# Output projection by seven block products with adding loads, one list schedule behind the attention, and a plain first feed-forward pair

## The chip, the cores and the metric

The kernel runs on one core of a Trainium2 chip. The metric is the device time of one execution in microseconds, as the median of several runs. The engines are TensorE (PE in the profile, with its weight loads as PEld), VectorE (DVE), ScalarE (ACT), GpSimd (POOL) and SyncE (SP), which here only issues transfers.

## The reference

One block of a network with two mixers, a 1024 x 1024 input in float32: an input projection, an mLSTM and a sparse attention side by side, and then what the change touches:

```python
branch = jnp.einsum('btnw,nwd->btnd', ys, w_branch[l])      # 2 branches, 512 -> 1024
gates = jax.nn.sigmoid(merge.reshape(B, T, N_BRANCH, D_MODEL))
mixed = jnp.sum(gates * branch, axis=2)
h = h + mixed @ w_out[l]                                    # 1024 x 1024
f = rms_norm(h, g_norm_ffn[l])
h = h + (jax.nn.silu(f @ w_gate[l]) * (f @ w_up[l])) @ w_down[l]   # 1024 -> 2816 -> 1024
return rms_norm(h, g_final)
```

## The kernel before

Every float32 product is made of three: both operands are split into a rounded part and a rest (hi by a copy on ACT, lo by a subtraction on another engine), and `mm3` (L350 to L353) issues hi x hi, hi x lo and lo x hi into one PSUM tile of 128 x 512. A plain product over 1024 inputs is thus 8 x 3 = 24 matmuls; a block product over 512 inputs is 12.

The attention ends at about 689 us of the trace, in the same way before and after the change. What follows it stood in two parts. The first is written out in order: three last tiles of the merge gates (`merge_tile`, matmuls on tile `d`), loads of the two mixers' results `y` and their splits (`load_y`), and the branch products (tile `br`, eight steps d of two halves and two branches; L1865 multiplies a product with its gate, L1873 adds the two branches, L347 and L348 split the sum into `UTH` and `UTL`, the eight mixed tiles). Their weights come through `Stream` (`ws`), which splits a weight tile on ACT (L331) and DVE or, for the merge gates, GpSimd (L333).

The second part is a list schedule (`Plan`): steps are recorded with the engines that may run them, an estimated cost and the buffers that they read and write. Then a greedy planner takes, again and again, the step that can start first, among the next few steps (`LOOK`) of each engine's list, and issues it. The costs are only the planner's; they set the order in which each engine's instructions stand in the program. Recorded there were: 16 output products `wout` (half of the columns, row block i; 24 matmuls each, and each reads all eight mixed tiles), each followed by the addition of x, a store of h and a square on ACT; `feats`, the normalisation of a row block (`rstd_steps`, small operations of one column, then L2000 with three operands) and its transposes (L2037); `fsplit`, the operands of the feed-forward's block products; `product`, the gate and up products by seven block products for each pair of 128-column tiles (m is a pair of tiles, q = 1, 2, 6, 7, 5, 4, 3 the product), the first pair with its four earliest products in halves of 256 columns; the down projection, by seven block products in two groups, with `combine` adding the products up on DVE or GpSimd; and a final stage (L2334), which does the last tiles of the down projection plainly, adds, normalises and stores. `ew` (L1893) records every element-wise operation, so in the profile all of them have that line, and they are told apart by their tiles; `act` is L1896, `dma` L1903. In the block products of gate and up one operand sum is made by a load that adds to what lies there (`sums`, L2109, issued by GpSimd), 256 KB each.

## Time and profile before

| | us |
|---|---|
| median of 3 runs | 1563.68 (1561.17 to 1564.3) |
| profiled execution | 1560.07 |
| its span in the trace | 1558.3 |
| TensorE busy | 1519.5 (98%), 7714 matmuls |
| DVE busy | 1159.7 (74%) |
| ACT busy | 782.0 (50%) |
| GpSimd busy | 182.2 (12%) |
| TensorE's part of the chain that ended last | 87% |

The part behind the attention is the last 869 us of the span. A stretch is read by comparing the busy time of TensorE with its length; a name such as `PS<-UTH,wh` gives the tile written and the tiles read. In the profile one matmul of 128x512 is shown with 0.39 us, which overlaps its neighbours; what it costs is the distance from one start to the next.

### The profile page before, as it was taken

How to read it: one execution, taken by the hardware profiler on the slowest of the kernel's cores; microseconds unless marked ns; L12 is line 12 of the kernel's file. 1: busy time of each engine (PE TensorE's matmuls, PEld its weight loads, DVE VectorE, ACT ScalarE, POOL GpSimd, SP SyncE). 2: the span in 40 equal slices, each digit the busy share in tenths (PEclk: the TensorE clock that was granted, in tenths of full speed). 3: DMA queues.
4: the chain of work that ended last, by engine and by line, in shares of the span. 5: the costliest groups of instructions: out<-in, count | busy, mean ns of one | idle time of the engine just before them, and what ended most of it. 6: DMA issues, size and time to landing. Idle time of an engine off the chain costs nothing.

```text
span 1558.3 us, 22160 instructions
## 1 busy us (share of the span) xinstructions
PE 1519.5 (98%) x7714; PEld 1283.8 (82%) x7714; DVE 1159.7 (74%) x2444; ACT 782.0 (50%) x1668; POOL 182.2 (12%) x235
## 2 busy tenths in 40 slices
PE   6999999999999999999999999999999999999997
PEld 5877888888989888987878888888888888888876
DVE  6978888875988688856564586666666666978996
ACT  5325665653888688865443353333333333454443
POOL 2000000013121412111000051000000000000120
PEclk9999999999999999999999999999999999999999
DMA  8324655489241925236455244444454443660202
GB/s 275 121 76 127 231 171 169 158 242 258 42 114 41 183 42 116 46 110 218 139 182 203 68 127 117 111 112 110 108 165 117 115 111 122 249 217 1 108 1 108
DMA packets 185496, 207.66 MB, mean 133 GB/s; under 512 B 10584, under 2 KB 145142, under 8 KB 185384
## 3 DMA queue, kind: packets, MB, share of 16 engines
q1 hardware_dynamic: 157272, 184.63, 37.4%
q0 software_dynamic: 27824, 20.96, 9.6%
q8 instruction: 61, 1.00, 0.3%
q10 hardware_dynamic: 288, 0.66, 0.1%
q14 instruction: 51, 0.42, 0.1%
HBM read 155.78 MB, written 58.29 MB: 137 GB/s over the span
## 4 chain that ended last, share of the span: by engine, by line
PE 87%; DVE 7%; DMA 3%; ACT 2%; issue 1%; SPq 0%; POOL 0%; DVEq 0%; ACTq 0%; POOLq 0%
PE PS L352 15%; PE PS L353 15%; PE PS L351 15%; PE bk L351 5%; PE bk L352 5%; PE bk L353 5%; PE T L1524 4%; PE obank L1546 2%; PE obank L1544 2%; PE d L351 2%; PE d L353 2%; PE d L352 2%; PE br L353 2%; PE br L352 2%; PE br L351 1%
## 5 line engine op out<-in xcount | busy, mean ns | idle before, releaser
L1893 DVE TENSOR_TENSOR sl<-PS,sl 128x512 f32<-128x512 f32 x182 | 123.1, 688 | 96.2 <-PE PS L353 93.5
L1533 DVE TENSOR_TENSOR TL<-T,TH 128x512 fp32r<-128x512 f32 (+1 forms) x184 | 103.3, 582 | 28.7 <-ACT TH L1529 27.8
L1529 ACT ACTIVATE TH<-T 128x512 fp32r<-128x512 f32 (+1 forms) x184 | 90.4, 510 | 26.2 <-PE T L1524 23.1
L1893 DVE TENSOR_TENSOR sl<-sl,sl 128x512 f32<-128x512 f32 (+1 forms) x113 | 77.7, 695 | 17.1 <-ACT sl L1896 13.3
L1896 ACT ACTIVATE sl<-sl 128x512 f32<-128x512 f32 (+1 forms) x85 | 53.2, 630 | 72.0 <-PE PS L352 46.8
L1896 ACT ACTIVATE wh<-sl 128x512 fp32r<-128x512 f32 x61 | 38.4, 630 | 80.4 <-PE PS L352 66.0
L351 PE MATMUL bk<-UTH,op 128*128 128x512 f32 x192 | 77.4, 403 | 0.0
L353 PE MATMUL bk<-UTH,op 128*128 128x512 f32 x192 | 75.0, 391 | 0.0
L352 PE MATMUL bk<-UTL,op 128*128 128x512 f32 x192 | 74.9, 390 | 0.0
L351 PE MATMUL d<-UTH,whi 128*128 128x512 f32 x176 | 71.8, 408 | 1.8 <-ACT mg L1396 1.1
L353 PE MATMUL d<-UTH,wlo 128*128 128x512 f32 x176 | 69.2, 393 | 0.8 <-POOL wlo L333 0.8
L352 PE MATMUL d<-UTL,whi 128*128 128x512 f32 x176 | 69.0, 392 | 0.0
L351 PE MATMUL PS<-q 128*128 128x512 f32 x172 | 66.9, 389 | 0.0
L352 PE MATMUL PS<-q 128*128 128x512 f32 x172 | 66.9, 389 | 0.0
L353 PE MATMUL PS<-q 128*128 128x512 f32 x172 | 66.9, 389 | 0.0
L1896 ACT ACTIVATE q<-sl 128x512 fp32r<-128x512 f32 x74 | 43.5, 625 | 45.7 <-PE PS L352 30.0
L351 PE MATMUL bk<-T,op 128*128 128x512 f32 x144 | 58.1, 404 | 0.0
L353 PE MATMUL bk<-T,op 128*128 128x512 f32 x144 | 56.3, 391 | 0.0
L352 PE MATMUL bk<-T,op 128*128 128x512 f32 x144 | 56.2, 390 | 0.0
L1558 POOL DMA_DIRECT2D d_yn<-os x32 | 31.9, 997 | 174.1 <-DMA d_yn<-os 51.1
L1893 DVE TENSOR_TENSOR wh<-sl,wh 128x512 fp32r<-128x512 f32 x59 | 40.4, 684 | 15.3 <-ACT wh L1896 15.3
L353 PE MATMUL br<-YH,wlo 128*128 128x512 f32 x128 | 49.9, 390 | 1.6 <-POOL wlo L333 1.6
(1378 smaller groups left out, 4898.3 us busy)
## 6 DMA issues: line engine op xcount, KB each, us to landing
rp<-in_w_in SPq DMA_DIRECT2D x22, 512.0 KB, 4.7
ra<-in_w_gate SPq DMA_DIRECT2D x22, 512.0 KB, 3.9
d_gu<-sl SPq DMA_DIRECT2D x44, 256.0 KB, 2.1
q<-d_mg SPq DMA_DIRECT2D x32, 256.0 KB, 3.1
d_rep<-d_row SPq DMA_DIRECT2D x8, 960.0 KB, 7.4
sl<-d_gu SPq DMA_DIRECT2D x15, 512.0 KB, 4.1
sl<-in_w_down SPq DMA_DIRECT2D x15, 512.0 KB, 4.7
ra<-in_w_up SPq DMA_DIRECT2D x11, 512.0 KB, 3.6
```

The costliest lines, as they stand in the source:

```text
L351: nc.tensor.matmul(ps, ah, bh, start=first, stop=False)
L352: nc.tensor.matmul(ps, ah, bl, start=False, stop=False)
L353: nc.tensor.matmul(ps, al, bh, start=False, stop=last)
L1524: nc.tensor.transpose(pt[:, z, P * r:P * r + P], e, ident)
L1529: nc.scalar.activation(hl[0][:, 0:m], pt[:, 0:m], AF.Copy)
L1533: nc.vector.tensor_tensor(hl[1][:, 0:m], pt[:, 0:m], cast32(hl[0])[:, 0:m], ALU.subtract)
L1544: nc.tensor.matmul(po, vv, th[:, z, :], start=(st[1] == 0), stop=False)
L1546: nc.tensor.matmul(po, vv, tl[:, z, :], start=False, stop=(st[1] == st[2]))
L1558: low_half.append(lambda: nc.gpsimd.dma_start(dst, half(1), accum_op=ALU.add))
L1893: return pl.step(alts, lambda e: ENG[e].tensor_tensor(out_(), x(), y(), alu), reads, writes, **kw)
L1896: return pl.step((("ACT", cost),), lambda e: nc.scalar.activation(out_(), x(), fn), reads, writes, **kw)
```

## The change

All that follows the attention is recorded in one `Plan`: merge tiles, loads of y, branch products, output projection, feed-forward. The planner looks further ahead (60 steps on PE in place of 10, 140 on DVE in place of 60), a step on PE is planned 1 us later than its operands, and element-wise steps go to DVE alone, apart from `combine` and the multiplies named below. The weights of merge and branches have their lo part made on DVE. The mixed rows stay whole (float32) in `UTH`.

The output projection is made by seven block products (`wprod(q, j)`, q = 1, 2, 6, 5, 3 and then 7 and 4 by turns, j the pair of row blocks; 28 steps of 12 matmuls). Its weight sums are made in memory order by loads: four plain ones (`wo_load`) and five adding ones on GpSimd (`wo_add`), 1 MB each, in three tiles (`quad_0` to `quad_2` in the order below); the sums of the mixed rows (`s1` to `s4`) are made on DVE; x comes by 16 adding loads of 256 KB on GpSimd (`xadd`), where it was loaded and added on DVE. The rows are normalised in pairs, and for 12 of the 16 tiles the multiplication with the gain is split: a scaled copy on ACT and a multiply on GpSimd. The first gate/up pair is made by eight plain products (`plain`), even rows first; the sums for the odd rows' block products follow (`row1_rest`).

```diff
-    pl = Plan([PS[:, n, :] for n in range(8)])
-    ENG = {"DVE": nc.vector, "Pool": nc.gpsimd}
-    ANY = (("DVE", 600.0), ("Pool", 1230.0))
-    V, SUM = (("DVE", 600.0),), (("DVE", 600.0),)
...
+    pl = Plan([PS[:, n, :] for n in range(8)], {"PE": 60, "SP": 60, "ACT": 100, "DVE": 140, "Pool": 60}, 1000.0)
+    ENG = {"DVE": nc.vector, "Pool": nc.gpsimd}
+    V = SUM = ANY = (("DVE", 670.0),)
+    V2 = (("DVE", 1140.0),)
+    BOTH = (("DVE", 670.0), ("Pool", 1230.0))
...
+    def dma(dst, src, reads=(), writes=(), kb=256.0, **kw):
+        pl.step((("SP", 400.0),), lambda e: nc.sync.dma_start(dst(), src()), reads, writes, kb=kb, nd=1, **kw)
+
+    def dma_add(dst, src, writes, lat):
+        pl.step((("Pool", 1000.0),), lambda e: nc.gpsimd.dma_start(dst(), src(), accum_op=ALU.add), (), writes, lat=lat)
...
+        if t:
+            rb = pl.buf(keys_of(raw), True)
+            if t > 1:
+                dma(lambda: v8(f32(raw)), lambda: src, (), [rb], kb=512.0)
+        hb, lb = pl.buf(keys_of(hi), True), pl.buf(keys_of(lo), True)
+        if t:
+            act(1000.0, lambda: slot_ap(hi, F32R), lambda: f32(raw), AF.Copy, [rb], [hb])
+            ew(V2, lambda: slot_ap(lo, F32R), lambda: f32(raw), lambda: cast32(slot_ap(hi, F32R)), ALU.subtract, [rb, hb], [lb])
+        wb[t] = [hb, lb]
...
+            m = [mxb.setdefault((d, r, h), pl.buf(ukeys("H", [d], [r], [2 * h, 2 * h + 1]), True)) if b == 0 else mxb[d, r, h] for r in range(2)]
+            if b == 0:
+                ew(V, lambda h=h: mixed(d, h), lambda ps=ps: ps.ap, lambda g=g: g.ap, ALU.mult, [ps, g], m)
+            else:
+                ew(V, lambda g=g: g.ap, lambda ps=ps: ps.ap, lambda g=g: g.ap, ALU.mult, [ps], [g])
+                ew(V, lambda h=h: mixed(d, h), lambda h=h: mixed(d, h), lambda g=g: g.ap, ALU.add, [g], m)
...
+    def wo_add(n, kh, ch):
+        b = WT[n]
+        dma_add(lambda: b.ap, lambda: wo_blk(kh, ch), [b], 12000.0)
...
+    HOME = {1: "L", 2: 0, 6: 8, 5: 0, 3: 8, 7: 20, 4: 0}
...
+    def prep_b(q, n):
+        t = WT[n]
+        for kk in range(4):
+            prepare(q, "B", kk, lambda kk=kk: t.ap[:, kk, :], [t])
...
+    def s3(kk):
+        ew(V, lambda: mx(kk, 1), lambda: mx(kk, 0), lambda: mx(kk, 1), ALU.subtract, mxs(kk, 0), mxs(kk, 1))
+
+    def s2(kk):
+        b = s2b[kk] = fpiece(28 + kk // 2, kk % 2)
+        stt_neg(lambda: four(b.ap), lambda: mx(kk, 1), lambda: mx(4 + kk, 1), mxs(kk, 1) + mxs(4 + kk, 1), [b])
+
+    def s1(kk):
+        b = s2b[kk]
+        stt_neg(lambda: mx(kk, 0), lambda: four(b.ap), lambda: mx(kk, 0), [b], mxs(kk, 0))
+
+    def s4(kk):
+        b = s2b[kk]
+        stt_neg(lambda: mx(4 + kk, 0), lambda: four(b.ap), lambda: mx(4 + kk, 0), [b], mxs(4 + kk, 0))
...
+    def wprod(q, j, ps, first=True, last=True):
+        def go(e):
+            for kk in range(4):
+                aa, bb = opb[q, "A", kk][2], opb[q, "B", kk][2]
+                js = slice(P * j, P * j + P)
+                mm3(ps.ap, aa(0)[:, js], aa(1)[:, js], bb(0), bb(1), first and kk == 0, last and kk == 3)
+        pl.step((("PE", 12 * 226.7),), go, [x for w in "AB" for kk in range(4) for x in opb[q, w, kk][:2]], [ps])
...
-    def wout(hf, i):
-        ps = pl.buf()
-        cs = slice(P * i, P * i + P)
-
-        def go(e):
-            for k in range(KT):
-                wh, wl = wod[k - k % 2] if hf == 0 else (b.ap for b in wo1[k - k % 2:k - k % 2 + 2])
-                mm3(ps.ap, UTH[:, k, cs], UTL[:, k, cs], wh[:, k % 2, :], wl[:, k % 2, :], k == 0, k == KT - 1)
-        pl.step((("PE", 5184.0),), go, [mixb[i]] + ([wo0], wo1)[hf], [ps])
-        return ps
...
+    def xadd(r, c, j):
+        b = xp[r, c, j]
+        i = 2 * j + r
+        src = a["x"][P * i:P * i + P, 512 * c:512 * c + 512]
+        dma_add(lambda: b.ap, lambda: src, [b], 6000.0)
...
+            stt(lambda b=b: b.ap, lambda b=b: b.ap, i, lambda c=c: gFb.ap[:, c, :], [gFb], [b], r == 0 or j < 2)
...
+    def row0(j):
+        for c, pt in enumerate(rows_f(0, j)):
+            b = xp[0, c, j]
+            fsplit(1 + c, j, lambda pt=pt: four(pt.ap), [pt])
+            act(587.0, lambda b=b: b.ap, lambda pt=pt: pt.ap, AF.Copy, [pt], [b])
...
+    def plain(m, r, c):
+
+        ps = pl.buf()
+        fq = ((1, 2), (8, 3))[r]
+
+        for kh in range(2):
+            def go(e, kh=kh):
+                o, (fh_, fl_) = OB[m, kh, c], blk(fq[kh])
+                for k in range(4):
+                    mm3(ps.ap, o.ap[:, 0, P * k:P * k + P], o.ap[:, 1, P * k:P * k + P], fh_[:, k], fl_[:, k], kh + k == 0, kh * k == 3)
+            pl.step((("PE", 12 * 226.7),), go, [OB[m, kh, c]] + [fsb[fq[kh], j] for j in range(4)], [ps])
...
-    seq = [(0, 1), (0, 2), (1, 1), (1, 2)]
-    seq += [(m, q) for q in (6, 7, 5, 4, 3) for m in (0, 1)]
-    seq += [(m, q) for m in range(2, NM) for q in (1, 2, 6, 7, 5, 4, 3)]
+    seq = [(m, q) for m in range(2, NM) for q in (1, 2, 6, 7, 5, 4, 3)]
...
+        if d == 0:
+            wo_load(0, 0, 0)
+            wo_load(1, 1, 1)
+            wo_load(2, 1, 0)
+        if d == 2:
+            for kk in range(4):
+                prep_a(1, kk)
+            prep_b(1, 0)
+            wo_add(0, 0, 1)
+            wo_add(0, 1, 1)
+            for kk in range(4):
+                s3(kk)
...
+    p1b += [x for w in "AB" for kk in range(4) for x in opb[1, w, kk][:2]]
+    b1 = bank()
+    for j in range(4):
+        wprod(1, j, b1[j])
+    for j in range(4):
+        out_piece(1, 0, j)
+        act(587.0, lambda d=xp[1, 0, j]: d.ap, lambda s=b1[j]: s.ap, AF.Copy, [b1[j]], [xp[1, 0, j]])
+    for kk in range(4):
+        s2(kk)
+        s1(kk)
+    prep_ab(2, 2)
+    wo_load(2, 0, 0)
+    wo_add(2, 0, 1)
+    b2 = bank()
+    for j in range(4):
+        wprod(2, j, b2[j])
+        out_piece(0, 0, j)
+        post(0, 0, j, b2[j], (1, 0))
+        xadd(0, 0, j)
...
+    prep_ab(6, 0)
+    wo_add(0, 1, 0)
+    plain_ops(0)
...
+    b6 = bank()
+    for j in range(4):
+        wprod(6, j, b6[j])
+        post(1, 0, j, b6[j])
+        stored(0, 0, j)
+    prep_ab(5, 2)
+    b5 = bank()
+    for j in range(4):
+        wprod(5, j, b5[j])
+        out_piece(1, 1, j)
+        post(1, 1, j, b5[j], (1, 0), 3)
+        xadd(1, 0, j)
+    prep_ab(3, 1)
+    wo_add(1, 0, 1)
+    b3 = bank()
+    for j in range(4):
+        wprod(3, j, b3[j])
+        out_piece(0, 1, j)
+        post(0, 1, j, b3[j], (1, 1), 2)
+        xadd(0, 1, j)
+        xadd(1, 1, j)
...
+    for j in range(4):
+        stored(0, 1, j)
+    for j in range(4):
+        b7 = pl.buf()
+        wprod(7, j, b7)
+        post(1, 1, j, b7, None, 2)
+        post(1, 0, j, b7)
+        stored(1, 1, j)
+        row0(j)
+        b4 = pl.buf()
+        wprod(4, j, b4)
+        post(1, 0, j, b4)
+        stored(1, 0, j)
+    plain_ops(1)
+    for j in range(4):
+        row1(j)
+    pl.boost = 80
+    for m in range(2):
+        for c in range(2):
+            plain(m, 0, c)
+    pl.boost = 0
+    for m in range(2):
+        for c in range(2):
+            plain(m, 1, c)
...
-                into(ANY, g(d), g(d), g(x), ALU.add, [g(x)])
-
+                into(BOTH, g(d), g(d), g(x), ALU.add, [g(x)])
```

GpSimd from the attention's last store on, before: weight splits of the merge tiles (`wlo`) and then element-wise work of the first feed-forward products (`wl`, `wh`).

```order
L1558 DMA d_yn_150<-os_7523 64x2x128
L333 TENSOR_TENSOR wlo_7568<-raw_6897,whi_7567 128x1024
L333 TENSOR_TENSOR wlo_7653<-raw_7548,whi_7652 128x1024
L333 TENSOR_TENSOR wlo_7734<-raw_7631,whi_7733 128x1024
L1893 TENSOR_TENSOR wl_8415<-ra_8411,wl_8415 128x512
L1893 TENSOR_TENSOR wh_8414<-ra_8412,wh_8414 128x512
L1893 TENSOR_TENSOR wh_8413<-ra_8410,wh_8413 128x512
```

After:

```order
L1560 DMA d_yn_150<-os_7523 64x2x128
L1875 DMA quad_0_float_7549<-in_w_out 128x4x512 x3
L1875 DMA quad_2_float_7569<-in_w_out 128x4x512
L1875 DMA UTL_float_8419<-in_x 128x512 x5
L1875 DMA quad_1_float_7564<-in_w_out 128x4x512
L1875 DMA UTL_float_8419<-in_x 128x512 x11
L1862 TENSOR_TENSOR UTL_float_8419<-UTL_float_8419,ra_7545 128x512 x12
```

GpSimd's splits are gone; its queue now holds the adding loads, those of the weights among those of x, and then the 12 multiplies with the gain.

DVE where the branches end and the output projection begins, before: the multiplies of the last mixed tile (`q_5_0`), a split of w_out's weights, the last mixed tile's addition and split, and splits of the other half of w_out.

```order
L1865 TENSOR_TENSOR q_5_0_7535<-br_8364,q_5_0_7535 128x512
L1865 TENSOR_TENSOR q_5_0_7535<-br_8378,q_5_0_7535 128x512
L333 TENSOR_TENSOR q_3_5_8354<-raw_8392,q_1_5_8353 128x1024
L1873 TENSOR_TENSOR q_5_0_7535<-q_5_0_7535 128x512
L348 TENSOR_TENSOR UTL<-q_5_0_7535,UTH 128x512
L1893 TENSOR_TENSOR sl_10_8468<-ra_8410,sl_8_8464 128x1024
```

After (`quad_3` holds gates, `UTH_float` the mixed rows, `ra` an operand sum, `sl_11` and `sl_18` the second product's lo parts):

```order
L1862 TENSOR_TENSOR quad_3_float_7598<-PS,quad_3_float_7598 128x512
L2039 SCALAR_TENSOR_TENSOR UTH_float_7797<-ra_7544,UTH_float_7797 128x4x128
L1862 TENSOR_TENSOR UTH_float_7797<-UTH_float_7797,quad_3_float_7598 128x512
L1862 TENSOR_TENSOR sl_11_float32r<-UTH_float_7797,sl_7_float32r 128x512
L1862 TENSOR_TENSOR quad_3_float_7598<-PS,quad_3_float_7598 128x512
L1862 TENSOR_TENSOR sl_18_float32r<-quad_2_float_7569,sl_14_float32r 128x512
L1862 TENSOR_TENSOR UTH_float_7797<-UTH_float_7797,quad_3_float_7598 128x512
L1862 TENSOR_TENSOR sl_18_float32r<-quad_2_float_7569,sl_14_float32r 128x512
```

The first product's operands stand earlier in the list; between the last mixed tiles' multiplies and additions there are now sums and splits for the second product.

## Rows read from the trace of the kernel before

**Rows 1.** The page: busy time of the engines over the span, TensorE's granted clock in 40 slices (9 is full), and the engines' shares of the chain that ended last.

```profile
PE 1519.5 (98%) x7714; PEld 1283.8 (82%) x7714; DVE 1159.7 (74%) x2444; ACT 782.0 (50%) x1668; POOL 182.2 (12%) x235
...
PEclk9999999999999999999999999999999999999999
...
PE 87%; DVE 7%; DMA 3%; ACT 2%; issue 1%; SPq 0%; POOL 0%; DVEq 0%; ACTq 0%; POOLq 0%
```

**Rows 2.** Busy time by stretch behind the attention: the stretch and its length, then busy us (and instructions) of PE, PEld, DVE, ACT and POOL, the granted clock, DMA share and GB/s.

```profile
688.00:720.00 32.00, 30.69 (x137) 24.96 (x136) 14.39 (x17) 16.58 (x24) 5.76 (x3) 1.00 0.72 245
720.00:740.00 20.00, 18.41 (x82) 14.92 (x81) 11.23 (x14) 9.69 (x16) 2.36 (x1) 1.00 0.71 211
...
810.00:820.00 10.00, 7.83 (x35) 6.18 (x34) 8.18 (x10) 5.34 (x9) 0.00 (x0) 1.00 0.64 205
820.00:902.00 82.00, 82.00 (x384) 68.42 (x383) 42.26 (x90) 26.07 (x59) 5.18 (x4) 1.00 0.38 131
902.00:947.00 45.00, 42.90 (x245) 37.20 (x244) 39.34 (x63) 21.84 (x40) 23.93 (x17) 1.00 0.53 129
947.00:1328.00 381.00, 381.00 (x1683) 315.48 (x1682) 245.14 (x382) 127.07 (x207) 23.10 (x18) 1.00 0.43 118
1328.00:1475.00 147.00, 147.00 (x650) 121.74 (x649) 132.09 (x216) 69.89 (x122) 5.10 (x4) 1.00 0.39 144
1475.00:1512.00 37.00, 35.21 (x155) 28.50 (x153) 37.00 (x51) 14.45 (x26) 14.38 (x10) 1.00 0.07 29
1512.00:1550.30 38.30, 36.83 (x161) 30.15 (x161) 26.20 (x74) 14.83 (x40) 0.56 (x1) 1.00 0.23 83
1550.30:1558.30 8.00, 0.00 (x0) 0.00 (x0) 3.37 (x9) 0.93 (x3) 1.94 (x2) 0.72 0.35 131
```

**Rows 3.** TensorE's waits from 690 us to the end: the waiting matmul's tile and line, what it waited for, us in total, times, and the longest.

```profile
PE PS L351 <- DVE q L1865: 2.2, 1, 2.2
PE PS L352 <- DVE q L1893: 1.9, 1, 1.9
PE br L353 <- POOL wlo L333: 1.6, 1, 1.6
PE PS L352 <- DVE wl L1893: 1.2, 1, 1.2
PE PS L352 <- DVE UTL L1893: 1.2, 2, 1.0
PE PS L2037 <- DVE sl L1893: 0.9, 2, 0.5
PE d L353 <- POOL wlo L333: 0.8, 1, 0.8
```

**Rows 4.** Timeline of TensorE in the first gate/up pair, the products in halves of 256 columns: start, duration, instruction.

```profile
911.02 0.28 PE L353 MATMUL PS<-UTH,wh 128*128 128x256 f32 x1
911.14 0.28 PE L351 MATMUL PS<-UTH,wh 128*128 128x256 f32 x1
```

**Rows 5.** Loads: the group of adding loads on GpSimd (busy, mean ns of one, idle ahead of it), the medians from issue to landing of those and of a plain 512 KB load of w_out (count, KB, us), and two stretches of 1 us in which an adding load lands (columns as in rows 2).

```profile
L2109 POOL DMA_DIRECT2D sl<-in_w_up x11 | 14.6, 1331 | 157.7 <-DMA sl<-in_w_up 157.7
...
sl<-in_w_up POOLq DMA_DIRECT2D x11, 256.0 KB, 5.0
ra<-in_w_out SPq DMA_DIRECT2D x4, 512.0 KB, 4.8
...
1012.00:1013.00 1.00, 1.00 (x6) 0.84 (x5) 0.96 (x2) 0.00 (x0) 0.00 (x0) 1.00 0.93 131
1013.00:1014.00 1.00, 1.00 (x6) 0.84 (x5) 0.85 (x2) 0.63 (x1) 0.00 (x0) 1.00 1.13 141
```

**Rows 6.** Timeline of DVE and GpSimd in the down projection's additions: start, duration of the group, instruction and count; and the group of GpSimd's additions over the whole run (busy, mean ns, idle before).

```profile
1478.16 4.44 DVE L1893 TENSOR_TENSOR acc<-acc 128x512 f32<-128x512 f32 x4
1479.77 1.68 POOL L1893 TENSOR_TENSOR acc<-acc,acc 128x512 f32<-128x512 f32 x1 [0.63 <-DVE acc L1893]
1508.26 2.47 DVE L1893 TENSOR_TENSOR acc<-acc,PS 128x512 f32<-128x512 f32 x4
1509.01 2.55 POOL L1893 TENSOR_TENSOR acc<-acc,acc 128x512 f32<-128x512 f32 x2 [11.46 <-DVE acc L1893]
...
L1893 POOL TENSOR_TENSOR acc<-acc,acc 128x512 f32<-128x512 f32 x10 | 13.6, 1373 | 56.2 <-DVE acc L1893 56.2
```

**Rows 7.** The entry of the output projection: a load of w_out in the chain that ended last, and the split that DVE ran on landing (timeline).

```profile
802.01 6.94 DMA raw<-in_w_out
808.74 2.55 DVE L333 TENSOR_TENSOR q<-raw,q 128x1024 fp32r<-128x1024 f32 x2 [1.01 <-ACT q L331]
```

**Rows 8.** Timeline behind the last matmul: the last addition, its square, the first and the last small operations of the normalisation, and the last multiply.

```profile
1550.23 0.69 DVE L1893 TENSOR_TENSOR acc<-acc,PS 128x512 f32<-128x512 f32 x1 [1.32 <-PE PS L353]
1551.01 0.63 ACT L1979 ACTIVATE sq<-acc 128x512 bf16<-128x512 f32 x1 [0.73 <-DVE acc L1893]
1551.77 0.49 DVE L1987 TENSOR_TENSOR sml<-sml 128x1 f32<-128x1 f32 x1 [0.85 <-ACT sq L1979]
1553.17 0.15 DVE L367 TENSOR_SCALAR sml<-sml 128x1 f32<-128x1 f32 x1
1553.55 1.41 DVE L2000 SCALAR_TENSOR_TENSOR ra<-acc,sml,sl 128x512 f32<-128x512 f32 x2
```

More of the change, by code (lines that the diff above doesn't have):

```diff
@@ new lines, in body, with own, quad, slot_ap @@
+    WHI = [two(whi0), wpl.tile([P, 2, 512], F32R, name="wh1", tag="whi", bufs=2)]
+    WLO = [two(wlo0), wpl.tile([P, 2, 512], F32R, name="wl1", tag="wlo", bufs=2)]
+    def own(key, pool, shape, dt, tag):
+        if key not in held or held[key].dtype != dt:
+            held[key] = pool.tile([P, *shape], dt, name=f"{tag}_{len(held)}_{dt.name}", tag=tag, bufs=1)
+        return held[key]
+    def quad(n, dt):
+        return own(("q", n), q2p if n < 4 else q1p, (4, 512), dt, f"quad{n}")
+    def slot_ap(n, dt):
+        if n < 8:
+            return own(n, q2p, (2, 512), dt, f"sl{n}")
+        if n < 28:
+            q = quad(n // 2 - 4, dt)
+            return q[:, 2 * (n % 2):2 * (n % 2) + 2, :]
+        if n < 31:
+            return RAW[n - 28]
+        return (WHI, WLO)[(n - 31) // 2][(n - 31) % 2]
@@ new lines, in big, with f32, keys_of, half_keys @@
+    def big(n, dt):
+        return own(("u", n), utp, (16, 512), dt, ("UTH", "UTL")[n])
+    def f32(n):
+        return slot_ap(n, F32)
+    def keys_of(n):
+        if 8 <= n < 28:
+            return [("Q", 2 * n - 16 + z, j) for z in range(2) for j in range(4)]
+        return [(n, z) for z in range(2)]
+    def half_keys(n, z):
+        k = keys_of(n)
+        h = len(k) // 2
+        return k[h * z:h * z + h]
+    def slot_buf(n, dt=F32):
+        return pl.buf(keys_of(n), make=lambda: slot_ap(n, dt))
@@ new lines, in piece, with pieces, fpiece, ukeys @@
+    def piece(c):
+        n, z = divmod(c, 2)
+        return pl.buf(half_keys(n, z), make=lambda: slot_ap(n, F32)[:, z, :])
+    def pieces(n):
+        return [piece(2 * n + z) for z in range(2)]
+    def fpiece(n, z):
+        return pl.buf(half_keys(n, z), make=lambda: f32(n)[:, z, :])
+    def ukeys(e, ks, rs, js):
+        return [("U", e, k, r, j) for k in ks for r in rs for j in js]
+    pl = Plan([PS[:, n, :] for n in range(8)], {"PE": 60, "SP": 60, "ACT": 100, "DVE": 140, "Pool": 60}, 1000.0)
@@ new lines, in body @@
+    for t in range(2):
+        weights(t, w_src(t))
+    for k in range(2):
+        yload(k)
+    merge(MG1)
+    weights(2, w_src(2))
+    yload(2)
+    merge(MG1 + 1)
+    weights(3, w_src(3))
+    yload(3)
+    merge(MG1 + 2)
+    weights(4, w_src(4))
+    for k in range(4, 8):
+        yload(k)
+    for d in range(0, 8, 2):
+        for z in range(2):
+            branch(d + z, 0)
+        for z in range(2):
+            branch(d + z, 1)
+            if d + z < 6:
+                weights(5 + d + z, w_src(5 + d + z))
+        if d == 0:
[10 more added lines that the diff above has]
+                s3(kk)
```

516 lines of the change are left out of this document (272 added, 244 removed).

## The prediction

> **What bounds the kernel now.** I read the page's first lines, then busy time by stretch of the part that the change rewrites, then TensorE's waits in it, and last the timeline at three places. TensorE bounds: it is busy 1519.5 of 1558.3 us at a granted clock of full speed in every slice, and 87% of the chain that ended last lies on it [rows 1]. DVE has 74%. So only two things can move the end: how many matmuls TensorE has to do, and how long it stands idle between the attention's last matmul (about 689.4) and the last matmul of all (1550.2). The stretches [rows 2] show that most of that part is full: 82.00 of 82, 381.00 of 381 and 147.00 of 147 us. Idle lies at six places: 1.31 us at 688 to 720 (0.47 of it the end of the attention, which stays), 1.59 at 720 to 740, 2.17 at 810 to 820, 2.10 at 902 to 947, 1.79 at 1475 to 1512 and 1.47 at 1512 to 1550. That is 10.4 in all, 9.9 without the attention's end, and the list of waits names 9.8 of it [rows 3]: the largest is the first output product waiting for a split of the weights or of the mixed rows (2.2), then an operand sum late in the down projection (1.9), then two waits on GpSimd's weight split (1.6 and 0.8). A last 8 us lie behind the last matmul.
>
> **TensorE's own work.** 1683 matmuls of 128x512 fill 381.00 us [rows 2], so one takes 0.2264 to 0.2267 us; a 256-wide one follows the next at 0.12 [rows 4]. The output projection goes from 16 products of 24 matmuls to 28 steps of 12: 384 to 336, -48 x 0.2267 = -10.9 us. The first gate/up pair goes the other way: before 14 block products, four of them in two 256-wide halves (96 x 0.12 = 11.5 us) and ten whole (120 x 0.2267 = 27.2), 38.7 us; after 8 plain products of 24 matmuls, 192 x 0.2267 = 43.5: +4.8. The 64 transposes stay. Sum **-6.1 us**. All of it is on the path, since no other engine is full where it is saved: DVE has 42.26 of 82 us beside the projection [rows 2].
>
> **The old waits (-9.8).** Each has a reason that the change takes away. The two waits on GpSimd (2.4): the one instruction that ran there at 720 to 740, a 128x1024 weight split, took 2.36 us [rows 2]; now the split is on DVE, 1.28 us [rows 7], where 14.39 of 32 us are busy [rows 2], with loads and splits issued one to two tiles earlier. By my tally of DVE's new order the tightest weight tile of the branches is ready 1.5 us before TensorE gets to it. The entry of the projection (2.2 + 1.2 + 1.2, with the loads behind them): before, a load of w_out landed only at 802.01 + 6.94 = 808.95, and DVE ran two weight splits from 808.74 for 2.55 us [rows 7], with the last mixed tile's operations queued behind, and every output product needs all eight mixed tiles. Now the first block product reads only mixed tiles 0 to 3, prepared during branches 4 to 7; tiles 4 to 7 are first read by the second, 10.9 us later. The transposes' 0.9 and the 1.9 and 1.2 of the down projection hang on DVE's order: there the list now looks ahead further, and three final steps (8.2 us) stand ahead of the step whose operand was late. I take all 9.8 out here and put what comes in their place into the next part.
>
> **New waits (+2.9).** Call the first output matmul 0; a step of 12 matmuls is 2.72 us, a block product 10.9.
> (a) *1 MB adding loads.* The trace has only 256 KB ones: 1.33 us of GpSimd each, 5.0 us from issue to landing [rows 5]. While one lands the queues move 131 to 141 GB/s, 0.14 MB a us. The extra 0.75 MB then take 5.4 us, so about 11 us for one, and about 7.5 more (1 MB/0.14) for one right behind it. GpSimd issues the third sum of tile 0 and the sum of tile 2 back to back at 10.5 to 12, once the third product's operands are split from tile 0; the second lands at 29 to 30.5. The fourth product (starts at 32.6) needs it at about 31.4, for its split. Slack 1 to 2.4 us: cost 0 to 1, I take 0.5. The lower bound is the plain 512 KB load's 4.8 us [rows 5], no cost; the upper is four times the 256 KB time, 20 to 23 us each, landing at 54: a stall of 22 us (a rival below). The next adding load (issued at about 42, since it is queued on GpSimd behind five loads of x that wait for products) has 15 us to its use at 57. The 16 loads of x land, by my tally, on results that are read 6 us later or more.
> (b) *Entry into the feed-forward.* The last transposes of the even rows come at about 78.8; copy on ACT and subtraction on DVE put its operand at 80.9, TensorE has no other work from 80.1: 0.8.
> (c) *GpSimd beside DVE.* The 12 multiplies move to GpSimd between about 59 and 80. Beside GpSimd's adds, four DVE adds with both operands in SBUF took 4.44 us, four with one in PSUM 2.47 [rows 6]. What DVE does there is mostly eviction from PSUM; exposed are the eight small rstd pieces (0.15 to 0.49 us each [rows 8]), each of which can be held by one GpSimd multiply of 1.28 to 1.37. Against that DVE has about 16 of 21.8 us of work. I take +0.6, bounds 0 and 4.5.
> (d) *Tail of the down projection.* DVE was full there, 37.00 of 37 [rows 2]: behind the fifth product 10 combining adds of 1.11 (4.44/4 [rows 6]), four evictions (2.47) and two splits (1.2) make 14.8 us, against five steps of TensorE, 13.6. Now 8 stay on DVE: 12.6. Of 1.9 + 1.2 I leave 0.7. The 8 us behind the last matmul keep their form [rows 8]; rstd has five small operations in place of four: +0.2.
> (e) *Operand work of the output products.* DVE's list has 26 more additions from PSUM, 10 fewer in SBUF and 12 more three-operand ones: about +18 us, in a stretch where it had 40 us idle. No stall, but 0.1.
> Sum of (a) to (e): 0.5 + 0.8 + 0.6 + 0.9 + 0.1 = **2.9**; bounds 0 and 22 + 4.5.
>
> **Sum.** The profiled execution took 1560.07 us (span 1558.3): 1560.07 - 6.1 - 9.8 + 2.9 = 1547.1. The median of the runs shown is 1563.68, 3.6 above it, so **1551** on the median.
>
> **Rivals.** *1. GpSimd holds DVE at the normalised rows.* For: [rows 6], and the transposes of the even rows are the last thing ahead of the feed-forward. Against: a slack of 5 to 6 us and a list that puts evictions between. If all eight small pieces wait, 10 us less the slack: +4.5, 1555. The Trainium skill has a rule on this place ("SBUF — State Buffer", section "Who interferes with whom"): a DVE instruction with two SBUF inputs contends with a GpSimd one that reads SBUF, and whichever issues second waits for the whole of the other; with one input in PSUM it does not. The trace agrees, 4.44 us against 2.47 for four [rows 6]; by that rule, with every piece caught, it would be the 1555.
> *2. The idle only moves.* A longer lookahead changes which operation is late, not that DVE has bursts: 132.09 of 147 and 37.00 of 37 us [rows 2]. For each old wait another of its size: 1563.7 - 6.1 = 1557.6. Against: seven tenths of the old idle (7.0 of 9.8) has a cause that is gone by the order itself (GpSimd's split, the late load of w_out, all eight tiles needed at once).
> *3. The adding loads are slow (slower).* If a 1 MB adding load costs four times a 256 KB one (20 to 23 us), the fourth product stands for 22 us: 1551 + 22 = 1573. It decides from about 17 us a load (10.5 + 2 x 17 = 44.5, 13 us after the need), where the stall eats the gain. For: adding loads have their own price, 5.0 us for 256 KB where 512 KB of plain load took 4.8 [rows 5], so a load can be bound by its own chain and not by bytes. Against: part of the 5.0 is a fixed start, and the rows here are pieces of 2 KB where those of the 256 KB loads are 512 bytes, so there are no more pieces than before.
>
> **How the numbers follow.** Forecast 0.63; rival 1 0.17; rival 2 0.11 (0.03 of it so far up that it is within 0.2%, which is 3.1 us and about what a measurement of this kernel can tell from no change); rival 3 0.09 (0.06 slower, 0.03 where the stall just eats the gain). Faster 0.63 + 0.17 + 0.08 = 0.88; same 0.03 + 0.03 = 0.06; slower 0.06. The range: with no new wait at all 1547.8, and runs stray by 1 us: 1547. Upward it takes in rivals 1 and 2: 1557.6 and a stray: 1559. Outside are rival 3 and some 0.08 of tails.
>
> **What would show it.** Matmuls after the attention fill about 835 us in place of 841. Idle of TensorE there falls from 9.9 to about 3. The sum of tile 2 lands by 31 us after the first output matmul, and no wait of the fourth or fifth product on it exceeds 1 us. The wait ahead of the first plain product is about 1 us; if it is 4 or more, with GpSimd's multiply beside DVE's small operations, rival 1 holds. If the sum of TensorE's waits is 9 or more without one that stands out, rival 2. A wait of over 10 us on an adding load makes the forecast wrong, as would a TensorE clock below full speed after such a wait, or branch products that wait for weights on DVE.

## The result and the profile after

| | before | after |
|---|---|---|
| median of the runs | 1562.71 us (4 runs) | 1553.76 us (1551.8 to 1554.96, 4 runs) |
| ratio after/before | | 0.9941, interval 0.9924 to 0.9959 |
| profiled execution | 1560.07 | 1554.78 |
| its span | 1558.3 | 1553.0 |

The kernel is 9 us faster where 12.7 were forecast, inside the stated range. From the page after: busy time of the engines, the clock in 40 slices and the shares of the chain that ended last; they answer to [rows 1]:

```profile
PE 1516.0 (98%) x7642; PEld 1277.9 (82%) x7642; DVE 1174.5 (76%) x2464; ACT 803.4 (52%) x1708; POOL 194.4 (13%) x252
...
PEclk9999999999999999999999999999999999999999
...
PE 85%; DVE 6%; DMA 5%; ACT 2%; issue 1%; SPq 0%; POOL 0%; DVEq 0%; ACTq 0%; POOLq 0%
```

The clock row looks as it did before, though the clock fell once (place C): a slice is 39 us long, and the 1.7 us that this cost leave its mean at 0.96. That the clock was full before has to be read from the stretches of [rows 2].

TensorE has 72 instructions fewer: 96 halves of 256 columns are gone and 24 whole ones have come, -96 x 0.12 + 24 x 0.2267 = -6.1 us of work, as the forecast had it. Its busy time fell by only 3.5. Busy time by stretch after (columns as in [rows 2]):

```profile
690.00:828.00 138.00, 138.00 (x609) 114.25 (x610) 83.95 (x113) 60.75 (x91) 7.01 (x6) 1.00 0.71 216
828.00:848.00 20.00, 18.34 (x79) 14.30 (x78) 10.16 (x17) 8.91 (x20) 2.62 (x3) 1.00 0.97 228
848.00:868.00 20.00, 20.00 (x90) 16.55 (x89) 19.65 (x33) 12.15 (x23) 10.02 (x11) 1.00 0.74 127
868.00:912.00 44.00, 40.53 (x206) 33.27 (x205) 30.69 (x65) 34.13 (x73) 17.11 (x14) 1.00 0.48 134
912.00:1328.00 416.00, 415.98 (x1837) 344.16 (x1837) 271.39 (x426) 139.87 (x231) 25.68 (x20) 1.00 0.47 126
1328.00:1348.00 20.00, 19.06 (x84) 15.40 (x84) 18.15 (x30) 11.94 (x23) 0.00 (x0) 1.00 0.68 263
...
1468.00:1488.00 20.00, 17.89 (x76) 14.45 (x76) 20.00 (x22) 6.43 (x12) 12.57 (x8) 0.96 0.16 51
1488.00:1508.00 20.00, 20.00 (x86) 16.45 (x85) 20.00 (x30) 8.09 (x15) 7.08 (x6) 0.96 0.00 1
1508.00:1545.00 37.00, 37.00 (x164) 30.41 (x163) 27.35 (x79) 14.79 (x40) 2.73 (x3) 1.00 0.23 85
```

The whole of merge, branches and the entry of the output projection (690 to 828) is now without a gap: the six places of [rows 2] have become four. Idle is 1.66 us at 828 to 848, 3.47 at 868 to 912, 0.94 at 1328 to 1348 and 2.11 at 1468 to 1488: 8.2 us, where 9.9 were before and 2.9 were forecast. The two stretches around 1488 also show a granted clock of 0.96. The waits behind them (columns as in [rows 3]):

```profile
PE PS L354 <- DVE wlo L1862: 2.1, 1, 2.1
PE PS L2166 <- POOL UTL_float L1862: 1.6, 2, 0.9
...
PE PS L353 <- ACT UTH_float32r L1865: 1.1, 1, 1.1
PE PS L353 <- ACT sl_float32r L1865: 1.0, 1, 1.0
PE PS L354 <- DVE wl L1862: 0.9, 1, 0.9
PE PS L354 <- DVE quad_float32r L1862: 0.7, 1, 0.7
PE PS L354 <- DVE sl_float32r L1862: 0.5, 1, 0.5
```

**Place A, the fourth output product (842 us).** Timelines of GpSimd, ACT and DVE, one after the other (start, duration, instruction, idle ahead of it and what ended it):

```profile
819.75 2.58 POOL L1875 DMA_DIRECT2D quad_float<-in_w_out  x2 [56.07 <-DVE quad_float32r L1862]
824.63 0.88 POOL L1875 DMA_DIRECT2D UTL_float<-in_x  x1 [2.29 <-DVE UTL_float L1862]
...
839.55 0.63 ACT L2097 ACTIVATE sq<-UTL_float 128x512 bf16<-128x512 f32 x1 [6.86 <-DMA UTL_float<-in_x]
840.19 2.18 ACT L1865 ACTIVATE sl_float32r<-UTH_float 128x512 fp32r<-128x512 f32 x4
...
840.83 1.90 DVE L1862 TENSOR_TENSOR sl_float32r<-UTH_float,sl_float32r 128x512 fp32r<-128x512 f32 x3 [5.54 <-ACT sl_float32r L1865]
```

GpSimd issues two 1 MB adding loads at once, as forecast, and the first load of x behind them. That load took from 824.63 to 839.5, 14.9 us. A square on ACT waits for it for 6.86 us, and behind that square on ACT stand the splits of the fourth product's operands. The sum of tile 2 itself was there: it landed at 837.9, 28 us after the first output matmul, where the forecast had 29 to 30.5.

**Place B, the even rows' transposes (868 to 912).** DVE's small operations and the multiplies of GpSimd beside them, out of the timelines of DVE and GpSimd:

```profile
881.19 1.07 DVE L2111 TENSOR_TENSOR sml<-sml 128x2 f32<-128x2 f32 x1
882.29 0.16 DVE L2112 TENSOR_TENSOR sml<-sml 128x2 f32<-128x2 f32 x1
...
889.94 1.22 DVE L2112 TENSOR_TENSOR sml<-sml 128x2 f32<-128x2 f32 x1
...
880.94 1.30 POOL L1862 TENSOR_TENSOR UTL_float<-UTL_float,ra 128x512 f32<-128x512 f32 x1 [1.47 <-ACT UTL_float L2123]
...
887.36 3.78 POOL L1862 TENSOR_TENSOR UTL_float<-UTL_float,ra 128x512 f32<-128x512 f32 x3 [0.89 <-ACT UTL_float L2123]
```

What takes 0.16 us took 1.07 and 1.22 there. But ACT, too, has 34.13 of 44 us of work, more than DVE.

**Place C, the second group of the down projection (1468 to 1490).** Timelines of DVE, GpSimd and TensorE:

```profile
1478.31 3.48 DVE L1862 TENSOR_TENSOR UTH_float<-UTH_float 128x512 f32<-128x512 f32 x2
1481.70 3.46 DVE L1862 TENSOR_TENSOR UTL_float<-UTL_float,UTH_float 128x512 f32<-128x512 f32 x2
...
1485.69 0.68 DVE L1862 TENSOR_TENSOR wlo<-sl_float,wlo 128x512 fp32r<-128x512 f32 x1
...
1479.50 1.73 POOL L1862 TENSOR_TENSOR UTH_float<-UTH_float,UTL_float 128x512 f32<-128x512 f32 x1
...
1486.42 0.80 PE L354 MATMUL PS<-wlo,whi 128*128 128x512 f32 x1 [2.12 <-DVE wlo L1862]
1487.02 0.63 PE L355 MATMUL PS<-wlo,whi 128*128 128x512 f32 x1
1487.44 0.63 PE L353 MATMUL PS<-wlo,whi 128*128 128x512 f32 x1
```

Combining adds on DVE and GpSimd go hand in hand, most of them at 1.5 to 1.8 us each; seven on DVE, of which the fence shows the last four, fill 1473.5 to 1485.1, and the split `wlo` behind them is late. After the wait the matmuls follow each other at 0.42 us. Busy time in stretches of 1 us there:

```profile
1486.00:1487.00 1.00, 0.58 (x1) 0.50 (x2) 1.00 (x3) 0.60 (x1) 0.00 (x0) 0.64 0.00 0
1487.00:1488.00 1.00, 1.00 (x4) 0.79 (x3) 1.00 (x2) 0.43 (x2) 0.00 (x0) 0.50 0.00 0
1488.00:1489.00 1.00, 1.00 (x4) 0.81 (x3) 1.00 (x3) 1.00 (x3) 0.00 (x0) 0.50 0.00 0
1489.00:1490.00 1.00, 1.00 (x4) 0.76 (x4) 1.00 (x3) 1.00 (x3) 0.00 (x0) 0.66 0.00 0
```

The granted clock is at its lower level (1.2 GHz) for part of four microseconds: 0.36 + 0.50 + 0.50 + 0.34 = 1.7 us of TensorE's time lost, counted as busy. The wait of 2.1 us and the fall behind it cost 3.8.

### The profile page after: what moved, and what is told of

It is laid out like the page before. It is cut to its first block, busy times and chain, and to the rows that moved or that the text cites. A ratio compares the mean times of both kernels' runs of the same rounds, so it can differ in the third digit from the quotient of the medians.

```text
span 1553.0 us, 22069 instructions
## 1 busy us (share of the span) xinstructions
PE 1516.0 (98%) x7642; PEld 1277.9 (82%) x7642; DVE 1174.5 (76%) x2464; ACT 803.4 (52%) x1708; POOL 194.4 (13%) x252
## 4 chain that ended last, share of the span: by engine, by line
PE 85%; DVE 6%; DMA 5%; ACT 2%; issue 1%; SPq 0%; POOL 0%; DVEq 0%; ACTq 0%; POOLq 0%
PE PS L354 16%; PE PS L355 16%; PE PS L353 16%; PE bk L353 5%; PE bk L354 5%; PE bk L355 5%; PE T L1526 4%; PE obank L1548 2%; PE obank L1546 2%; PE d L353 2%; PE d L355 2%; PE d L354 2%; DMA UTL_float<-in_x 1%; DMA rp<-in_w_in 1%; DMA d_mg<-S 1%
## 5 line engine op out<-in xcount | busy, mean ns | idle before, releaser
L1862 DVE TENSOR_TENSOR UTL_float<-PS,UTL_float 128x512 f32<-128x512 f32 x144 | 97.3, 689 | 80.2 <-PE PS L355 79.2
L354 PE MATMUL PS<-quad_float32r,sl_float32r 128*128 128x512 f32 x240 | 93.4, 389 | 0.0
L353 PE MATMUL PS<-quad_float32r 128*128 128x512 f32 x196 | 76.3, 389 | 0.0
L355 PE MATMUL PS<-quad_float32r 128*128 128x512 f32 x196 | 76.3, 389 | 0.0
L354 PE MATMUL PS<-quad_float32r 128*128 128x512 f32 x196 | 76.3, 389 | 0.0
L354 PE MATMUL PS<-quad_float32r,whi 128*128 128x512 f32 x176 | 68.6, 390 | 0.7 <-DVE quad_float32r L1862 0.7
L354 PE MATMUL PS<-quad_float32r,wh 128*128 128x512 f32 x164 | 63.8, 389 | 0.0
L353 PE MATMUL d<-UTH,whi 128*128 128x512 f32 x128 | 53.1, 414 | 1.7 <-ACT mg L1398 1.5
L1865 ACT ACTIVATE quad_float32r<-quad_float 128x512 fp32r<-128x512 f32 x57 | 32.8, 622 | 41.3 <-PE PS L354 29.4
L354 PEld LDWEIGHTS PS<-quad_float32r,sl_float32r 128*128 128x128 f32 x240 | 45.1, 188 | 9.3
L355 PE MATMUL d<-UTH,wlo 128*128 128x512 f32 x128 | 50.4, 394 | 0.0
L353 PE MATMUL PS<-UTH_float32r,sl_float32r 128*128 128x512 f32 x124 | 48.4, 390 | 0.0
(1488 smaller groups left out, 4933.9 us busy)
```

The lines of the kernel that those rows point to most:

```text
L353: nc.tensor.matmul(ps, ah, bh, start=first, stop=False)
L354: nc.tensor.matmul(ps, ah, bl, start=False, stop=False)
L355: nc.tensor.matmul(ps, al, bh, start=False, stop=last)
L1862: return pl.step(alts, lambda e: ENG[e].tensor_tensor(out_(), x(), y(), alu), reads, writes, **kw)
L1865: return pl.step((("ACT", cost),), lambda e: nc.scalar.activation(out_(), x(), fn), reads, writes, **kw)
```

## The experiments

Times are medians, ratios against the kernel before on the same chip, which took 1560.0 to 1561.7 us there. They stand in four groups, each beside the kernel before on one chip: after_again, w4_late, mult_dve and comb_dve; w4_mult, w4_mult_c80, before_look and before_merge; w4_mult_b600, w4_mult_cc_spread and noadd; act_dve. Between groups the ratios count, not the times.

A second measure leaves the attention out: from the start of the first matmul behind it to the start of the last matmul of all, in the profiled executions. It is 860.5 us before (689.35 to 1549.80) and 854.8 after (689.93 to 1544.76), and is called *the part behind the attention* below. It is one execution each.

**after_again**: the changed kernel unaltered.

> The changed kernel once more, for the spread of its runs and their clocks: 1551 to 1556 us. If TensorE's clock falls to its lower level after the wait in the down projection in some runs only, the spans of the runs differ by the 1.7 us that this costs; if the spread of about 3 us has nothing to do with the clock, runs of one clock differ as much.

1554.82 us, ratio 0.9957 (0.9944 to 0.9970). The profiled run had the clock down twice, at place C and behind place B. Mean clocks of six runs: 0.995 to 0.999, and the fastest run (1551.98) is the one with 0.999. The kernel before ran at 0.996 to 0.999 too; its profiled execution, at 0.999, was one without a fall and below the median. So clock falls explain part of the spread of both. Runs of one clock still differ, by 1.2 to 1.6 us here and by up to 2.9 in the kernel before. A part of that lies ahead of the change: the first matmul behind the attention starts at 688.39 in the trace of mult_dve and at 690.63 in that of w4_mult, both at a mean clock of 0.997, though no edit reaches what stands ahead of it. Why it does stays open.

**w4_late**: place A.

```diff
     prep_ab(6, 0)
-    wo_add(0, 1, 0)
...
         post(1, 0, j, b6[j])
         stored(0, 0, j)
+    wo_add(0, 1, 0, [xp[0, 0, 3]])     # planned behind the fourth load of x
```

> The third sum of weight tile 0 (1 MB, not needed before the last block product) is issued on GpSimd behind the first four loads of x instead of ahead of them. Theory: the 2.3 us that TensorE stands ahead of and in the fourth output product come from ACT, whose splits for that product stand behind a square that waits 6.9 us for the first adding load of x, and that load stands behind two 1 MB adding loads in the queue. Then the load lands some 7 us earlier, ACT's wait falls below 1 us, TensorE's idle at that place below 0.5, and the kernel is 2 us faster than the changed one. Rival: ACT is simply full there with squares and eight splits; then at least 1.5 us of the idle stay. Second rival: the load only moves the queue, and the sum of tile 1 or the later loads of x land later: what is won there is lost 20 us on, no change.

1548.32 us, ratio 0.9921 (0.9908 to 0.9934): 6.5 below the changed kernel. The square got its x at 835.1 in place of 839.55, 4.4 us earlier and not 7, and no wait of TensorE is left at this place. ACT's wait for it did not fall below 1 us, it rose from 6.86 to 9.47, since ACT came to it earlier. ACT in the changed kernel (the square is shown at place A), and then in this one:

```profile
831.54 0.63 ACT L1865 ACTIVATE wlo<-ra 128x512 fp32r<-128x512 f32 x1 [8.62 <-DMA ra<-in_w_gate]
...
824.48 0.63 ACT L1865 ACTIVATE wlo<-ra 128x512 fp32r<-128x512 f32 x1 [1.08 <-DMA ra<-in_w_gate]
...
835.10 0.63 ACT L2097 ACTIVATE sq<-UTL_float 128x512 bf16<-128x512 f32 x1 [9.47 <-DMA UTL_float<-in_x]
```

So the edit did more than its theory said. A plain 512 KB load of the first pair's weights (`ra<-in_w_gate`, issued by SyncE at 820.7 in the changed kernel and at 820.9 here) ended ACT's wait 7 us earlier, with one large adding load beside it and not two. In the changed kernel DVE's splits of it held the second product's additions back, so that the next three loads of x were issued only at 834.4 to 835.6; here they went out at 827.8 to 833.2. ACT was not full there, so that rival falls; the later loads of x did not give the gain back. The gain is larger than the 1.7 us of idle: idle at place B went from 3.47 to 2.17 (868 to 912) as well, and the part behind the attention is 850.9, 4.0 less than in the changed kernel, with one fall of the clock in either (here at B, a clock of 0.96 in that stretch, and none at C). The rest of the 6.5 lies in runs that were not profiled; the profiled one is the slowest of the four.

**mult_dve**: place B.

```diff
-            stt(..., [gFb], [b], r == 0 or j < 2)
+            stt(..., [gFb], [b], False)
```

> The 12 multiplies of the normalised rows with their gain go back from ACT and GpSimd to one three-operand instruction each on DVE. Theory: the 4.2 us that TensorE waits around the transposes of the even rows come from the way over ACT (0.72 us) and GpSimd (1.27 us), and from GpSimd holding DVE's small operations (1.07 and 1.22 us where 0.16 is usual); then that idle falls to about 1.5 and the kernel is 2 to 3 us faster than the changed one. Rival: the normalisation starts late because the squares wait for the adding loads of x, and nothing behind them matters: no change within 0.5 us. A third: DVE gets 9 us more in a stretch of 30 where it was busy about two thirds of the time, and the waits move to its splits: up to 2 us slower.

1550.51 us, ratio 0.9930 (0.9917 to 0.9942): 4.3 below after_again; the part behind the attention is 852.1, 2.7 below the changed kernel's. TensorE's busy time at 868 to 912, this kernel:

```profile
868.00:912.00 44.00, 42.69 (x216) 35.09 (x214) 37.45 (x81) 30.51 (x64) 0.45 (x1) 1.00 0.44 127
```

Idle there fell from 3.47 to 1.31, with waits for DVE and ACT left; in after_again that stretch also held a clock fall. DVE carries 37.45 us and is not the new bound.

**comb_dve**: place C.

```diff
-                into(BOTH, g(d), g(d), g(x), ALU.add, [g(x)])
+                into(V, g(d), g(d), g(x), ALU.add, [g(x)])
```

> All combining adds of the down projection on DVE, none on GpSimd. Theory: DVE and GpSimd hold each other up (DVE's adds with both operands in SBUF took 1.5 to 1.77 us beside GpSimd and 0.6 alone), so that the eight adds on DVE and the twelve on GpSimd take the 13 us that twenty on DVE alone would need (12.2): the wait of 2.3 us and the clock's fall behind it (1.6 us) shrink or go, 1.5 to 4 us faster than the changed kernel. Rival: DVE is the bound of that stretch by its amount of work, and 7 us more on it make the wait longer: 3 to 6 us slower.

1554.15 us, ratio 0.9957 (0.9943 to 0.9971): as the changed kernel. DVE's sixteen adds ahead of the late split took 9.6 us alone (0.6 each) where seven had taken 11.6 beside GpSimd, but two waits of 1.8 and 0.9 stayed. So GpSimd's share had bought almost nothing, and its holding DVE up is not the whole cause of the wait; neither theory holds as stated.

**w4_mult**: the edits of w4_late and mult_dve together.

> Both edits at once: the third sum of weight tile 0 behind the first loads of x, and the 12 multiplies on DVE. If the two waits have causes of their own, both go: TensorE's idle of 2.3 us at the fourth output product and of 4.2 around the even rows' transposes, and with the second the clock's fall of 1.7 us; left are 1.1 us at the entry of the down projection and 2.3 to 4 in its second group. About 1546 us, 8 to 9 below the changed kernel. Rival: an earlier start only meets the same late loads of x and ACT's queue, so that the second edit brings nothing on top of the first: 1548.

1546.68 us, ratio 0.9910 (0.9893 to 0.9926). Between 868 and 912 TensorE is busy 43.95 of 44 us, and place A is clean. In the traces the two edits add up: idle at 868 to 912 is 3.47 in the changed kernel, 2.17 with w4_late, 1.31 with mult_dve and 0.05 with both, and the part behind the attention is 4.0, 2.7 and 6.9 us shorter. The medians do not show it: by the ratios this kernel is 0.1% below w4_late, within the intervals, so that by time alone the rival (nothing on top) is not out. Left are the waits of the down projection, 0.9 and 2.1, and the clock fall behind the second.

**w4_mult_c80**: w4_mult with the adds ranked later.

```diff
+                pl.boost = -80
                 into(BOTH, g(d), g(d), g(x), ALU.add, [g(x)])
+                pl.boost = 0
```

> As the kernel before it in this call, and the combining adds get a rank 80 steps later in the plan, so that splits of the next product's operands stand ahead of them on DVE. Theory: the wait of 2.3 us in the second group of the down projection is one of order, a split queued behind 13 us of adds: it falls below 0.5, the clock's fall behind it goes, 2 to 4 us less than without, about 1543. Rival: the adds are needed by the final stage, and DVE has no room for them later: the wait comes back there with 2 us or more.

1551.54 us, ratio 0.9944 (0.9930 to 0.9959), 4.9 worse. The wait came back later and larger, as the rival said in the main; it had put it in the final stage, and it came about one product later:

```profile
PE PS L354 <- DVE wh L1862: 5.5, 1, 5.5
```

**before_look**: the kernel before with `Plan([...], {"PE": 60, "SP": 60, "ACT": 100, "DVE": 140, "Pool": 60}, 1000.0)`.

> The kernel before with nothing but the changed kernel's lookahead and its 1 us of slack for TensorE in the plan. If the plan's longer sight were what pays, the idle at the first gate/up pair (2.7 us) and in the down projection (3.5 us) would fall by half or more: 3 us faster than before. If it only changes which operation is late, the sum of those waits stays within 1.5 us of 6.2 and the time within 0.15%.

1562.72 us, ratio 1.0019 (1.0009 to 1.0028): slower by 0.2%. The down projection got better (TensorE busy 39.79 of 40 us at 1468 to 1508), the first gate/up pair worse: 39.13 of 45 at 902 to 947 with a clock of 0.89, against 42.90 in [rows 2]. A wait there, in which the clock fell:

```profile
PE PS L2037 <- DVE sl L1893: 3.5, 1, 3.5
```

A longer look ahead alone moves the idle and gains nothing.

**before_merge**: the kernel before, `pool=j < MG1` for `pool=True` in `merge_tile`.

> The kernel before with the weight splits of the last three merge tiles on DVE in place of GpSimd. Theory of the forecast: the two waits on GpSimd's split (1.0 and 1.75 us in the starts of the matmuls) go and nothing takes their place: 2.5 us faster, 0.16%. Rival: DVE's splits of y are held up by it, and another wait of 1 to 2 us appears in the same stretch: no change.

1557.39 us, ratio 0.9985 (0.9976 to 0.9994): 2.6 faster. Both waits on GpSimd's split ([rows 3], 1.6 and 0.8) are gone and no wait has come in that stretch. This term of the forecast held, alone as in the change.

**w4_mult_b600**: place C again.

```diff
-    BOTH = (("DVE", 670.0), ("Pool", 1230.0))
+    BOTH = (("DVE", 600.0), ("Pool", 1230.0))
```

> The kernel with both edits (third sum of tile 0 later, multiplies on DVE), and the plan's cost of a combining add on DVE back at 600 ns from 670, as it was before the change; nothing else. Theory: the cost sets how many of the twenty adds behind the fifth product GpSimd gets (more in the changed kernel), and each of GpSimd's adds holds one of DVE's, so the split behind them comes late; with fewer on GpSimd the wait of 2.3 us becomes 0.5 to 1.4 as it was before, and the clock's fall behind it (1.7) goes with it: 1543 to 1545. Rival: the stretch holds more work than DVE can do either way, and the wait stays at 2 or more: 1546.7.

**1544.18 us**, ratio 0.9896 (0.9880 to 0.9913), faster than both kernels; all four runs had a mean clock of 0.999. Groups of GpSimd's combining adds from 1400 us on, in the changed kernel and then in this one:

```profile
L1862 POOL TENSOR_TENSOR UTL_float<-UTL_float,UTH_float 128x512 f32<-128x512 f32 x10 | 14.3, 1463 | 39.3 <-DVE UTH_float L1862 22.9 <-DVE UTL_float L1862 16.3
L1862 POOL TENSOR_TENSOR UTH_float<-UTH_float 128x512 f32<-128x512 f32 x7 | 11.0, 1596 | 158.8 <-DVE UTH_float L1862 158.7
L1862 POOL TENSOR_TENSOR UTH_float<-UTH_float,UTL_float 128x512 f32<-128x512 f32 x3 | 4.3, 1442 | 10.3 <-DVE UTL_float L1862 10.3
```

```profile
L1862 POOL TENSOR_TENSOR UTL_float<-UTL_float,UTH_float 128x512 f32<-128x512 f32 x7 | 9.2, 1339 | 41.0 <-DVE UTH_float L1862 24.6 <-DVE UTL_float L1862 16.3
L1862 POOL TENSOR_TENSOR UTH_float<-UTH_float 128x512 f32<-128x512 f32 x5 | 7.7, 1549 | 162.0 <-DVE UTH_float L1862 162.0
L1862 POOL TENSOR_TENSOR UTH_float<-UTH_float,UTL_float 128x512 f32<-128x512 f32 x3 | 4.3, 1447 | 11.1 <-DVE UTL_float L1862 11.1
```

Twenty adds on GpSimd (w4_mult has twenty as well) have become fifteen (before the change fourteen), the wait 2.1 has become 1.3, and the clock does not fall. The planner's guess of 70 ns had sent five adds to the engine that holds DVE up. Against w4_mult that is 0.14% by the ratios, about 2 us, with intervals that overlap; the part behind the attention is 845.6 against 847.9.

**w4_mult_cc_spread**: w4_mult with `BOTH` at 1300 and 1700 and the adds regrouped (`7: ((7, 1),), 5: ((8, 5), (5, 1)), 6: ((7, 6), (5, 6), (8, 7))`).

> The same two edits, with the combining adds of the fifth product taken apart so that eight of twenty can be done behind the third and fourth (the first product is added to the third and fourth there, the sixth later; four adds more in all), and planned at 1300 and 1700 ns, about what they take on DVE and GpSimd side by side. Theory (a burst at one place): the wait in the second group falls below 0.5, the clock does not fall, 1542 to 1544. Rival (DVE's total): it is full over the whole stretch, four adds more make the waits longer, 1547 or more.

1551.14 us, ratio 0.9940 (0.9926 to 0.9955): as the rival had it. One wait of 5.1 us at the same place, with a clock fall. DVE is busy 77.5 of 80 us at 1420 to 1500. Regrouping, four adds more and other costs came in one edit here, so which of them made the wait longer is not shown.

**noadd**: the adding loads as plain ones on GpSimd's queue, so the weight sums and the addition of x are left out.

> The changed kernel with the adding loads of w_out and x as plain loads on the same GpSimd queue: the sums of the weights and the addition of x are left out. One look at the landing times. If adding is what costs, a 1 MB load lands in 6 us or less where the adding one took 11.3, and x's first load in 6 to 7 where it took 14.9, and TensorE's 2.3 us at the fourth product go. If it is the bytes in the queue, the landings stay within 2 us of those.

One execution, 1549.41 us. Medians from issue to landing at 745 to 870, in the changed kernel and then in this one:

```profile
quad_float<-in_w_out POOLq DMA_DIRECT2D x5, 1024.0 KB, 11.3
UTL_float<-in_x POOLq DMA_DIRECT2D x16, 256.0 KB, 8.8
```

```profile
quad_float<-in_w_out POOLq DMA_DIRECT2D x5, 1024.0 KB, 6.0
UTL_float<-in_x POOLq DMA_DIRECT2D x16, 256.0 KB, 4.4
```

So it is the adding, and not the bytes alone, that makes these loads slow. The doubling of the 256 KB median is in part a wait behind the others: with nothing ahead on the queue a load of x landed after 4.0 us adding (issued at 852.83) and 2.9 plain (at 847.06), a 1 MB load after 11.3 and 8.9 adding and 7.0 and 6.0 plain. The bytes count too: ACT still waits 6.2 us for the plain load of the gate weights here, where it waited 8.6. TensorE has no wait at place A in this kernel.

**act_dve**: w4_mult_b600 with the scaled copy on ACT as in the change and the multiply behind it on DVE.

> The best kernel so far (third sum of tile 0 later, combining adds planned at 600 ns), but with the 12 multiplies with the gain made in two steps again: the scaled copy on ACT stays, and the multiply is on DVE, not on GpSimd. It tells which half of the way cost the wait around the even rows' transposes. If it was ACT's scaled copies (12 x 0.72 us on an engine that was busy 34 of 44 us there), TensorE's idle between 868 and 912 comes back to 1.5 us or more and the clock may fall: 1546 to 1548. If it was GpSimd (its 1.27 us, and DVE's small operations held by it), the idle stays below 0.5 us: 1544 to 1545, as with one instruction on DVE.

1546.36 us, ratio 0.9907 (0.9887 to 0.9927), 2.2 above w4_mult_b600 by the median and 1.7 by the part behind the attention (847.3). Busy time at 868 to 912:

```profile
868.00:912.00 44.00, 42.33 (x218) 35.26 (x217) 39.16 (x85) 37.20 (x78) 0.35 (x1) 1.00 0.39 120
```

Idle is back at 1.67 us, with waits of 0.9 for DVE and 0.8 for ACT, without GpSimd. Of the 3.47 us at place B, 1.3 came from place A: w4_late left 2.17. Of these 2.17, the scaled copies on ACT (37.20 of 44 us busy) and the extra operation each bring back 1.67. GpSimd's share is then about 0.5 us and what the clock lost in some of the executions; it was not separated further.

## Why the prediction was right, and which term was not

The sign, the range and the first term held: by the count of matmuls TensorE's work fell by 6.1 us, and this alone is most of the gain. Of the old waits, the 2.4 on GpSimd's splits, the 2.2 at the projection's entry and the 2.1 at the first pair went (690 to 828 is full; before_merge shows the first of them alone). Two waits of 1.2 that the forecast put at the projection's entry were not there: in the trace of before one lies at the first gate/up pair and one in the down projection. With one 1.2 counted twice, the waits named there add up to 11.0, while the sum took 9.8; and of the "seven tenths" of the old idle whose cause the order takes away, 4.6 of 9.8 are left. The 1.9 and 1.2 of the down projection did not go; 2.1 and 0.9 stand in their place. The longer look ahead did take them out in the kernel before (before_look, 39.79 of 40 us), but with fourteen adds on GpSimd, not twenty.

The step that failed is the sum of the new waits, 2.9. It measured 8.2 us of idle and 1.7 of clock in the profiled execution.
- *(a), 0.5.* The landing of a 1 MB adding load (11.3 us against "about 11") was right, and so was the issue of two at once. Wrong was the sentence that the loads of x land 6 us ahead of their readers: the first stood behind both and took 14.9 us, and its reader is a square that holds the fourth product's splits on ACT. It cost 1.7 of idle, and w4_late took it out. That the two large loads would also hold back a plain weight load from another queue, and with it ACT and DVE, was not in the forecast.
- *(b) and (c), 1.4.* 3.5 measured. Rival 1 has its mechanism in the trace (0.16 us became 1.07 and 1.22), but the forecast counted DVE's slack and not ACT's, which got 12 scaled copies (mult_dve, act_dve).
- *(d), 0.9.* 3.1 of idle measured, and the clock. The forecast took fewer adds on DVE as a relief. They cost more each: 11.6/7 = 1.66 us in place of 1.11, since nearly each of DVE's had one of GpSimd's beside it. The Trainium skill ("SBUF — State Buffer", section "Who interferes with whom") says that a DVE instruction with two SBUF inputs and a GpSimd one that reads SBUF shut each other out; the seven that took 11.6 us, and the sixteen that took 9.6 alone, agree. The forecast had quoted that rule for place B; here it took 1.11 from four adds that had one of GpSimd's beside them [rows 6], and counted eight at that price. That is not the whole: without GpSimd's adds comb_dve still waits 2.7 us, which points to DVE's amount of work beside the price of one.
- *The clock* was named as a way to be wrong and had no price: 1.7 us in this execution.

By mechanism, the profiled execution is close to rival 2 (the idle only moves): 1560.07 - 6.1 = 1554.0 against 1554.78, and the part behind the attention is 5.6 us shorter (3.8 in after_again, whose clock fell twice), where the rival has 6.1 and the forecast 13.0. The forecast's own sign for the rival, 9 us or more of waits, was just missed at 8.2. The medians gained 9.0 and 6.8 us, between the rival's 6.1 and the forecast's 12.7, and the two effects can't be told apart there to better than 2 us. That the time came out inside the range is thus owed to the width of the range, which took in the rival, and not to the term for the waits. That idle could be taken out and was not a law is shown by w4_mult_b600: with three small edits its waits behind 690 us are 2.2 us in all, and it is 16 to 17 us faster than the kernel before. Not explained is about 1 us of TensorE's busy time: 3.5 less and 1.7 of clock make 5.2, where 6.1 were to go.
